# S5 parameter arithmetic (exponentials, angle reduction, powers, unit rotations) issued on GpSimd in place of VectorE

## The chip, the cores and the metric

The kernel runs on one core of a Trainium2 chip. A core has a matrix engine (TensorE; PE in the profile, its weight loads PEld), and three engines for elementwise work: VectorE (DVE), ScalarE (ACT) and GpSimd (POOL); SyncE (SP) issues the DMAs used here. Each engine runs its own instructions strictly in order and waits on semaphores where it needs another engine's result. The metric is the device time of one launch in microseconds (us), lower is better.

## The reference

The program is a trunk of two residual layers over 1024 tokens of width 1024. Layer 0 projects the RMS-normalised input once and runs two branches on it: sliding-window attention with RMS-normalised queries and keys, and an S5 state-space layer. Layer 1 is a sparse attention with a top-k indexer. The change touches only the parameters of S5, which are 32 groups x 64 states:

```
dt = exp(log_dt)[:, None]
mag = exp(a_re * dt)
ang = a_im * dt
ab_re = mag * cos(ang);  ab_im = mag * sin(ang)
den = a_re * a_re + a_im * a_im
f_re = ((ab_re - 1) * a_re + ab_im * a_im) / den
f_im = (ab_im * a_re - (ab_re - 1) * a_im) / den
bb_re = f_re * b_re - f_im * b_im;  bb_im = f_re * b_im + f_im * b_re
x = associative_scan(a complex recurrence with ab over the tokens, driven by bb u)
y = Re(c x) + d_skip * u
```

## The kernel before, in words

All S5 parameters lie as 128 partitions x 16 columns (two states to a partition group), so each elementwise step on them is one instruction on a 128x16 tile. `exp_of` is an exponential written out as elementwise steps: clamp, split off the power of two with a magic constant, range reduction, a polynomial, a rebuilt exponent; 14 instructions on VectorE. It is called twice, for `dt` and, after `tt = a_re*dt`, for `mag`. `ang` is reduced to `r` in [-pi, pi] (`k`, then three fused steps, then a clamp); ScalarE takes sin of `r` and of pi/2-|r|. From `mag`, cos and sin come `P5`, `pw` (the recurrence's factor and its squares) and `ue`, seven unit rotations, each the `square` of the one before, brought back to length one by `unit`. `T16` is built from `ue[0..3]`, `Bb` from `P5`, and both start the S5 quarters (`Q`, `Tb`, `W`, `M`, `X`), the first of which the matrix engine needs at L649.

Around it runs the start of layer 0. Eight pieces of x (1024 tokens x 128) come in by DMA. For each, ScalarE makes `hT_hi` (L335), VectorE the remainder `hT_lo` (L336), and PE multiplies both with the first weights (L356 to L358). The squares (ScalarE, L340) are summed into `acc` (L342), on GpSimd for the first two pieces and on VectorE for the other five. Then one chain leads to the RMS factor of every token:

- PE sums `acc` over partitions (L207), VectorE adds eps (L208), GpSimd raises to -1/2 (L209, `rr`);
- VectorE spreads `rr` on a diagonal (L364, `sq`), PE broadcasts it (L367), ScalarE copies it (L368, `rb`).

PE next projects keys and values, 8 row blocks (L216 to L218, `mm` tiles in three PSUM buffers). Each block's two key heads are normalised by `norm_heads`: squares on ScalarE (L388), then on GpSimd eps (L199), power (L200), factor `rr` (L392); ScalarE scales (L394), which frees the `mm` buffer, and GpSimd applies the gain (L396). Then comes the second chunk of S5's input projection, `u_chunk(1)` (L230 to L232). Weights are split in a high part (ScalarE, L153) and a low part (`wlo`, L154, on VectorE or on GpSimd).

The order of each engine's instructions is fixed when the program is built: a scheduler simulates the program as written, with the `high_priority` blocks first, and writes one list for each engine. The lists decide the rest: an instruction that waits holds all behind it on its engine.

Of the kernel before, what the change touches and what calls it, by code (L numbers as in the profile page):

```python
# [8 lines left out]
F32 = mybir.dt.float32  # L9
# [5 lines left out]
OP = mybir.AluOpType  # L15
# [44 lines left out]
def bc(ap, shape):  # L60
    return ap.to_broadcast(shape)
# [7 lines left out]
def tile_hybrid_swa_s5_dsa(  # L69
# [5 lines left out]
    V, S, G, T = nc.vector, nc.scalar, nc.gpsimd, nc.tensor  # L75
# [159 lines left out]

    MAGIC = 12582912.0

    def exp_of(sp, o, xin, n):

        a, kf, pl = (sp.tile([128, n], F32, name=f"ex{i}", bufs=2) for i in range(3))  # L240
        ki = sp.tile([128, n], I32, name="exi", bufs=2)
        V.tensor_scalar(a, xin, 88.0, -87.0, op0=OP.min, op1=OP.max)
        V.tensor_scalar(kf, a, 1.0 / math.log(2.0), MAGIC, op0=OP.mult, op1=OP.add)
        V.tensor_scalar(kf, kf, MAGIC, None, op0=OP.subtract)
        V.scalar_tensor_tensor(a, kf, -0.693359375, a, op0=OP.mult, op1=OP.add)
        V.scalar_tensor_tensor(a, kf, 0.693359375 - math.log(2.0), a, op0=OP.mult, op1=OP.add)
        V.tensor_scalar(pl, a, 1.0 / 5040.0, None, op0=OP.mult)
        for d_ in (720.0, 120.0, 24.0, 6.0, 2.0, 1.0):
            V.scalar_tensor_tensor(pl, pl, 1.0 / d_, a, op0=OP.add, op1=OP.mult)
        V.tensor_scalar(ki, kf, 127.0, 8388608.0, op0=OP.add, op1=OP.mult)  # L250
        V.scalar_tensor_tensor(o, pl, 1.0, ki.bitcast(F32), op0=OP.add, op1=OP.mult)


    g1r_d = dr.tile([8, FZ], F32, name="g1r_d")
# [41 lines left out]
    sp = es_sp.enter_context(tc.tile_pool(name="s5p", bufs=1, side="right", reuse_waits="tile"))  # L296

    def q16(name):
        return sp.tile([128, 16], F32, name=name)
# [3 lines left out]
    ldt = q16("ldt")  # L303
    with tc.tile_pool(name="x0", bufs=1, reuse_waits="tile") as xp:
# [26 lines left out]
        for k in range(8):  # L331
            xt = xts[k]
            for c in range(0, L, 512 if k == 0 else L):
# [3 lines left out]
                                       op0=OP.mult, op1=OP.subtract)  # L337
# [14 lines left out]
            for half in range(2):  # L352
                for f in range(2):
                    o, hs = ups[2 * f + half], slice(half * 512, half * 512 + 512)
                    a, b = w[0][:, k, f * 128:(f + 1) * 128], w[1][:, k, f * 128:(f + 1) * 128]
# [77 lines left out]
    pw = s5.tile([128, 3, 2, 16], F32, name="pw")  # L433
# [4 lines left out]
    with es_sp:  # L438
        Bre, Bim = Bt[:, 0], Bt[:, 1]
        are, aim = aa[:, 0], aa[:, 1]  # L440
        dt = q16("dt")
        exp_of(sp, dt, ldt, 16)
        tt, ang, k, r = q16("tt"), q16("ang"), q16("k"), q16("r")
        mag, cs, sn, fre, fim = (P5[:, i, :] for i in range(5))
        V.tensor_mul(tt, are, dt)
        exp_of(sp, mag, tt, 16)
        V.tensor_mul(ang, aim, dt)
        V.tensor_scalar(k, ang, 1.0 / (2 * math.pi), MAGIC, op0=OP.mult, op1=OP.add)
        V.tensor_scalar(k, k, MAGIC, None, op0=OP.subtract)
        c1 = 6.28125  # L450
        c2 = 0.0019350051879882812
        c3 = 2 * math.pi - c1 - c2
        V.scalar_tensor_tensor(r, k, -c1, ang, op0=OP.mult, op1=OP.add)
        V.scalar_tensor_tensor(r, k, -c2, r, op0=OP.mult, op1=OP.add)
        V.scalar_tensor_tensor(r, k, -c3, r, op0=OP.mult, op1=OP.add)
        V.tensor_scalar(r, r, 3.1415925, -3.1415925, op0=OP.min, op1=OP.max)
        S.activation(sn, r, AF.Sin)
        V.scalar_tensor_tensor(tt, r, -1.0, r, op0=OP.mult, op1=OP.max)
        V.tensor_scalar(tt, tt, -1.0, math.pi / 2, op0=OP.mult, op1=OP.add)
        S.activation(cs, tt, AF.Sin)  # L460
        den, nre, nim = q16("den"), q16("nre"), q16("nim")
        V.tensor_mul(den, are, are)
        V.tensor_mul(tt, aim, aim)
        V.tensor_add(den, den, tt)
        V.reciprocal(den, den)
        V.tensor_mul(nre, mag, cs)
        V.tensor_scalar(nre, nre, -1.0, None, op0=OP.add)
        V.tensor_mul(nim, mag, sn)
        V.tensor_mul(fre, nre, are)
        V.tensor_mul(tt, nim, aim)  # L470
        V.tensor_add(fre, fre, tt)
        V.tensor_mul(fre, fre, den)
        V.tensor_mul(fim, nim, are)
        V.tensor_mul(tt, nre, aim)
        V.tensor_sub(fim, fim, tt)
        V.tensor_mul(fim, fim, den)
        G.memset(CB, 0.0)
        dma(CT, sc_in)
        V.tensor_scalar(CT[:, 1], CT[:, 1], -1.0, None, op0=OP.mult)


        dma(dsk[96:128], bass.AP(tensor=sd_in.tensor, offset=sd_in.offset, ap=[[0, 32], [1, 512]]))
        dv = dsk[96:128].rearrange("h (q i g) -> h q i g", q=4, g=8)
        GE.tensor_mul(dv, dv,
                      bc(ident[96:128, None, 112:128, None], [32, 4, 16, 8]))

        tm = [sp.tile([128, 256], F32, name=f"tm{i}") for i in range(4)]

        def small(i):
            return tm[i][:, :16]  # L490

        mg, c_, s_ = P5[:, 0], P5[:, 1], P5[:, 2]
        V.tensor_mul(pw[:, 0, 0], mg, c_)
        V.tensor_mul(pw[:, 0, 1], mg, s_)

        def square(dst, src):
            V.tensor_mul(small(0), src[:, 0], src[:, 0])
            V.tensor_mul(small(1), src[:, 1], src[:, 1])
            V.tensor_sub(dst[:, 0], small(0), small(1))
            V.scalar_tensor_tensor(dst[:, 1], src[:, 0], 2.0, src[:, 1], op0=OP.mult, op1=OP.mult)  # L500

        square(pw[:, 1], pw[:, 0])
        square(pw[:, 2], pw[:, 1])
        square(ue[:, 0], P5[:, 1:3])
        square(ue[:, 1], ue[:, 0])
        square(ue[:, 0], ue[:, 1])

        def unit(e):

            V.tensor_mul(small(0), e[:, 0], e[:, 0])  # L510
            V.tensor_mul(small(1), e[:, 1], e[:, 1])
            V.tensor_add(small(0), small(0), small(1))
            V.tensor_scalar(small(0), small(0), -0.5, 1.5, op0=OP.mult, op1=OP.add)
            V.tensor_mul(e, e, bc(small(0)[:, None, :], [128, 2, 16]))

        unit(ue[:, 0])
        for i in range(1, 7):
            square(ue[:, i], ue[:, i - 1])
            unit(ue[:, i])
        V.memset(T16[:, 0, :, 0:1], 1.0)  # L520
        V.memset(T16[:, 1, :, 0:1], 0.0)
        for lv in range(4):
            n = 1 << lv
            er, ei = (bc(ue[:, lv, i, :, None], [128, 16, n]) for i in range(2))
            ts = [t[:, :16 * n].rearrange("p (j n) -> p j n", n=n) for t in tm]
            V.tensor_mul(ts[0], T16[:, 0, :, 0:n], er)
            V.tensor_mul(ts[1], T16[:, 1, :, 0:n], ei)
            V.tensor_mul(ts[2], T16[:, 1, :, 0:n], er)
            V.tensor_mul(ts[3], T16[:, 0, :, 0:n], ei)
            V.tensor_sub(T16[:, 0, :, n:2 * n], ts[0], ts[1])  # L530
            V.tensor_add(T16[:, 1, :, n:2 * n], ts[2], ts[3])
        V.tensor_mul(R8, mg, mg)
        V.tensor_mul(R8, R8, R8)
        V.tensor_mul(R8, R8, R8)
        fr, fi = (bc(P5[:, i, :, None], [128, 16, 16]) for i in (3, 4))
        tmv = [t.rearrange("p (j h) -> p j h", h=16) for t in tm]
        V.tensor_mul(tmv[0], Bre, fr)
        V.tensor_mul(tmv[1], Bim, fi)
        V.tensor_sub(Bb[:, 0], tmv[0], tmv[1])
        V.tensor_mul(tmv[2], Bim, fr)  # L540
        V.tensor_mul(tmv[3], Bre, fi)
        V.tensor_add(Bb[:, 1], tmv[2], tmv[3])
# [264 lines left out]
    for u in range(16 + SWA_AHEAD):  # L807
        if u < 16:
            b, kv = divmod(u, 2)
# [5 lines left out]
        if u >= SWA_AHEAD:  # L815
            b, kv = divmod(u - SWA_AHEAD, 2)
# [39 lines left out]
    for i in range(2):  # L856
        whi, wlo = wstream.get()
        wstream.after = ()
        for half in range(2):
            t0 = half * 512  # L860
            ca = cat[half]
            for n2 in range(2):
                n = 2 * i + n2
                pp = []
                for part in (1, 0):
                    ps = ps_mm.tile([128, 512], F32, name="mm")
                    for k in range(4):
                        a = whi[:, 2 * k + part, n2 * 128:(n2 + 1) * 128]
# [6 lines left out]
                sg = st3.tile([128, 512], F32, name="sg", bufs=4)  # L875
# [18 lines left out]
    for half in range(2):  # L894
# [20 lines left out]
        r = xp1.tile([128, 4], F32, name="r1")  # L915
# [16 lines left out]
    for k in range(0, 8, 3):  # L932
        n = min(3, 8 - k)
# [699 lines left out]
```

## Time and profile before

| what | value |
|---|---|
| median of 3 runs | 1088.2 us (1085.74 to 1091.84) |
| profiled execution | 1088.23 us; its span 1086.5 us, 1.7 us around it |
| busy PE / DVE / ACT / POOL | 1020.1 / 792.8 / 597.2 / 445.9 us |
| TensorE clock granted, mean | 0.976 |

Busy time is the sum over an engine's instructions; the span is from the first to the last instruction of the core. Times in rows count from the start of the span.

### The profile page before, as it was taken

The page shows a single profiled execution, that of the slowest core. Times are in us where ns is not written, and L with a number is a line of the kernel's source. Part 1 is how long each engine was busy: PE and PEld are TensorE (multiplying, and loading weights), DVE is VectorE, ACT ScalarE, POOL GpSimd, SP SyncE. Part 2 cuts the span into 40 slices and gives each one's busy share as a digit, 9 for nine tenths or more (in the row PEclk, how much of TensorE's full clock was granted, in tenths as well). Part 3 has the DMA queues.
Part 4 walks back from the last instruction along what each step waited for, and adds up shares of the span by engine and source line. Part 5 has one row for each costly group of instructions (what it writes and reads, how often), then busy time and mean ns, then how long its engine had stood idle before and what let it go on. Part 6 is the DMA issues. An engine that isn't in the chain of part 4 may idle for free.

```text
span 1086.5 us, 19104 instructions
## 1 busy us (share of the span) xinstructions
PE 1020.1 (94%) x6536; PEld 895.5 (82%) x6536; DVE 792.8 (73%) x1758; ACT 597.2 (55%) x1589; POOL 445.9 (41%) x650
## 2 busy tenths in 40 slices
PE   6898899999999899999799989999997879999998
PEld 4697889999777488878589989999886768988898
DVE  7899798636778554386668578988896988777742
ACT  6453455225546332254455889789935866665520
POOL 2167795232212022144140578767413455445000
PEclk9899899999999999999999999999998999999999
DMA  7283454474323416542012122112336785655323
GB/s 262 78 266 97 128 152 112 148 233 146 116 89 126 136 58 198 199 148 95 1 40 69 64 80 84 40 64 87 105 104 210 224 252 168 194 182 170 106 94 120
DMA packets 109074, 142.52 MB, mean 131 GB/s; under 512 B 9609, under 2 KB 84233, under 8 KB 104113
## 3 DMA queue, kind: packets, MB, share of 16 engines
q1 hardware_dynamic: 108976, 141.31, 41.2%
q8 instruction: 51, 0.84, 0.3%
q14 instruction: 47, 0.38, 0.1%
HBM read 104.41 MB, written 38.31 MB: 131 GB/s over the span
## 4 chain that ended last, share of the span: by engine, by line
PE 68%; DVE 18%; ACT 4%; DMA 4%; issue 3%; POOL 3%; SPq 1%; DVEq 0%; ACTq 0%; POOLq 0%
PE mm L230 8%; PE mm L231 8%; PE mm L232 8%; PE mm L216 4%; PE mm L217 4%; PE mm L218 4%; PE mm L1505 2%; PE mm L1506 2%; PE mm L1504 2%; PE tr L1373 2%; PE psx L799 2%; DVE xh L925 1%; PE pq L1347 1%; DVE tmp L690 1%; PE mm L1388 1%
## 5 line engine op out<-in xcount | busy, mean ns | idle before, releaser
L154 POOL TENSOR_TENSOR wlo<-wraw,whi 128x512 fp32r<-128x512 f32 (+1 forms) x42 | 90.3, 2176 | 104.3 <-ACT whi L153 98.5
L153 ACT CAST whi<-wraw 128x512 fp32r<-128x512 f32 (+2 forms) x120 | 83.7, 755 | 71.8 <-PE mm L231 27.6
L1346 POOL TENSOR_TENSOR bt<-bt,mk 128x384 f32<-128x384 f32 (+3 forms) x80 | 85.0, 1077 | 81.6 <-DMA bt<-g_d 54.6
L216 PE MATMUL mm<-whi,h1T_hi 128*128 128x256 f32 x384 | 110.3, 289 | 0.0
L218 PE MATMUL mm<-whi,h1T_lo 128*128 128x256 f32 x384 | 109.7, 287 | 0.0
L217 PE MATMUL mm<-wlo,h1T_hi 128*128 128x256 f32 x384 | 109.6, 286 | 0.0
L1207 DVE TENSOR_SCALAR_CACHE_REDUCE vjunk<-sc,vt 128x512 bf16<-128x512 uint16 (+5 forms) x90 | 91.1, 1012 | 3.0
L231 PE MATMUL mm<-hT_lo,whi 128*128 128x256 f32 (+1 forms) x288 | 86.3, 300 | 0.0
L232 PE MATMUL mm<-hT_hi,wlo 128*128 128x256 f32 (+1 forms) x288 | 86.3, 300 | 0.0
L230 PE MATMUL mm<-hT_hi,whi 128*128 128x256 f32 (+1 forms) x288 | 85.9, 298 | 0.0
L1241 ACT ACTIVATE sjunk<-sc,st 128x384 bf16<-128x384 uint16 (+5 forms) x90 | 77.3, 859 | 6.4 <-POOL st L1245 4.1
L154 DVE TENSOR_TENSOR wlo<-wraw,whi 128x512 fp32r<-128x512 f32 (+1 forms) x78 | 58.7, 787 | 23.4 <-ACT whi L153 19.1
L1504 PE MATMUL mm<-aT_hi,whi 128*128 128x256 f32 x256 | 73.4, 287 | 1.2 <-ACT aT_hi L1478 1.2
L216 PEld LDWEIGHTS mm<-whi,h1T_hi 128*128 128x128 f32 x384 | 73.1, 191 | 0.6
L1505 PE MATMUL mm<-aT_lo,whi 128*128 128x256 f32 x256 | 72.6, 283 | 0.9 <-DVE aT_lo L1479 0.9
L217 PEld LDWEIGHTS mm<-wlo,h1T_hi 128*128 128x128 f32 x384 | 73.1, 190 | 0.3
L218 PEld LDWEIGHTS mm<-whi,h1T_lo 128*128 128x128 f32 x384 | 72.9, 190 | 0.3
L1506 PE MATMUL mm<-aT_hi,wlo 128*128 128x256 f32 x256 | 72.4, 283 | 0.0
L394 ACT ACTIVATE st<-mm,nr 128x64 f32<-128x64 f32 (+1 forms) x160 | 45.5, 357 | 40.8 <-POOL nr L392 36.7
L1357 ACT ACTIVATE s<-s,mn 128x128 f32<-128x128 f32 (+7 forms) x64 | 49.5, 774 | 29.0 <-DVE mn L1351 29.0
L1064 DVE SCALAR_TENSOR_TENSOR sc<-relu,wi,sc 128x384 f32<-128x384 f32 (+3 forms) x70 | 49.5, 708 | 20.5 <-ACT relu L1059 16.6
L1376 ACT CAST pT_hi<-tr 128x512 fp32r<-128x512 f32 x72 | 41.3, 578 | 37.4 <-PE tr L1373 33.4
(383 smaller groups left out, 3493.4 us busy)
## 6 DMA issues: line engine op xcount, KB each, us to landing
wraw<-in_w_dram SPq DMA_DIRECT2D x20, 1024.0 KB, 5.1
wraw<-in_wo_dram SPq DMA_DIRECT2D x16, 1024.0 KB, 5.1
bt<-g_d SPq DMA_DIRECT2D x24, 256.0 KB, 3.8
g_d<-g1r_d SPq DMA_DIRECT2D x8, 576.0 KB, 10.8
bt<-g_d SPq DMA_DIRECT2D x24, 192.0 KB, 3.5
qT_d<-gst SPq DMA_DIRECT2D x32, 128.0 KB, 2.3
qT<-qT_d SPq DMA_DIRECT2D x32, 128.0 KB, 3.4
xh<-in_xT_dram SPq DMA_DIRECT2D x16, 256.0 KB, 3.2
```

The source lines that it names most:

```text
L154: eng.tensor_sub(lo[p_], raw[p_], rd(hi[p_]))
L216: T.matmul(ps, a, hi[:, k, c0:c1], start=(k == 0), stop=False)
L217: T.matmul(ps, a, lo[:, k, c0:c1], start=False, stop=False)
L218: T.matmul(ps, b, hi[:, k, c0:c1], start=False, stop=(k == 7))
L230: T.matmul(o, a, hT[0][:, k, ts], start=(k == 0), stop=False)
L231: T.matmul(o, a, hT[1][:, k, ts], start=False, stop=False)
L232: T.matmul(o, b, hT[0][:, k, ts], start=False, stop=(k == 7))
L1207: V.tensor_scalar(junk[:, :128 * (b + 1)], data(b), self.thr(j), None, op0=OP.is_ge, op1=OP.add, accum_out=self.cnt[:, it, j:j + 1])
L1346: G.tensor_add(bt, bt, mk[b][:, ks])
L1504: T.matmul(ps, a, aT[0][:, k, toks], start=(k == 0), stop=False)
L1505: T.matmul(ps, a, aT[1][:, k, toks], start=False, stop=False)
L1506: T.matmul(ps, b, aT[0][:, k, toks], start=False, stop=(k == 7))
```

## The change

`exp_of` gets the engine and a fused-step function as arguments, and both calls now run on GpSimd. A fused step (scalar_tensor_tensor), one instruction on VectorE, becomes two on GpSimd, which pass through one shared tile `stt_t`. So one exponential has 23 instructions in place of 14, and a `square` 5 in place of 4. Products with `dt`, the reduction of `ang`, the clamp, pi/2-|r|, `pw`, all `square` and all `unit` go to GpSimd too. |r|, `den`, `nre`, `nim`, `fre`, `fim`, `R8`, `T16` and `Bb` stay on VectorE.

```
-        exp_of(sp, dt, ldt, 16)
+        stt_t = q16("stt_t")
+
+        def g_stt(o, a, c, b, op0, op1):
+            G.tensor_scalar(stt_t, a, c, None, op0=op0)
+            G.tensor_tensor(o, stt_t, b, op=op1)
+
+        exp_of(G, g_stt, sp, dt, ldt, 16)
...
-        V.tensor_mul(tt, are, dt)
-        exp_of(sp, mag, tt, 16)
-        V.tensor_mul(ang, aim, dt)
+        G.tensor_mul(tt, are, dt)
+        exp_of(G, g_stt, sp, mag, tt, 16)
+        G.tensor_mul(ang, aim, dt)
...
-        V.scalar_tensor_tensor(r, k, -c1, ang, op0=OP.mult, op1=OP.add)
...
+        g_stt(r, k, -c1, ang, op0=OP.mult, op1=OP.add)
...
-        V.tensor_mul(pw[:, 0, 0], mg, c_)
-        V.tensor_mul(pw[:, 0, 1], mg, s_)
+        sg_ = [q16(f"sg{i}") for i in range(2)]
+        G.tensor_mul(pw[:, 0, 0], mg, c_)
+        G.tensor_mul(pw[:, 0, 1], mg, s_)
...
         def square(dst, src):
-            V.tensor_mul(small(0), src[:, 0], src[:, 0])
-            V.tensor_mul(small(1), src[:, 1], src[:, 1])
-            V.tensor_sub(dst[:, 0], small(0), small(1))
-            V.scalar_tensor_tensor(dst[:, 1], src[:, 0], 2.0, src[:, 1], op0=OP.mult, op1=OP.mult)
+            G.tensor_mul(sg_[0], src[:, 0], src[:, 0])
+            G.tensor_mul(sg_[1], src[:, 1], src[:, 1])
+            G.tensor_sub(dst[:, 0], sg_[0], sg_[1])
+            g_stt(dst[:, 1], src[:, 0], 2.0, src[:, 1], op0=OP.mult, op1=OP.mult)
...
         def unit(e):
...
-            V.tensor_mul(e, e, bc(small(0)[:, None, :], [128, 2, 16]))
+            G.tensor_mul(sg_[0], e[:, 0], e[:, 0])
+            G.tensor_mul(sg_[1], e[:, 1], e[:, 1])
+            G.tensor_add(sg_[0], sg_[0], sg_[1])
+            G.tensor_scalar(sg_[0], sg_[0], -0.5, 1.5, op0=OP.mult, op1=OP.add)
+            G.tensor_mul(e, e, bc(sg_[0][:, None, :], [128, 2, 16]))
```

The lists differ in the first eighth of the program only. GpSimd's list from the sums of squares to the first key norms, before:

```order
L342 TENSOR_TENSOR acc<-acc,sq 128x1024 x2
L209 TENSOR_TENSOR rr<-rr,neghalf 128x8
L199 TENSOR_SCALAR nr<-nms 128x2
L200 TENSOR_TENSOR nr<-nr,neghalf 128x2
L199 TENSOR_SCALAR nr<-nms 128x2
L392 TENSOR_TENSOR nr<-nr,rr 128x2
```

After the change the same list goes on, behind the second sum, with 72 steps of S5's parameters (both exponentials, `ang`, `r`, `pw`, the first `square` of `ue`); L445 and L446 are the two halves of a fused step. Its end, and what follows:

```order
L445 TENSOR_SCALAR stt_t<-P_386 128x16
L504 TENSOR_TENSOR ue<-sg_498,sg_499 128x16
L446 TENSOR_TENSOR ue<-stt_t,P_386 128x16
L209 TENSOR_TENSOR rr<-rr,neghalf 128x8
L502 TENSOR_TENSOR sg_498<-ue 128x16
L503 TENSOR_TENSOR sg_499<-ue 128x16
...
L518 TENSOR_SCALAR sg_498<-sg_498 128x16
L199 TENSOR_SCALAR nr<-nms 128x2
L519 TENSOR_TENSOR ue<-ue,sg_498 128x32
L200 TENSOR_TENSOR nr<-nr,neghalf 128x2
L199 TENSOR_SCALAR nr<-nms 128x2
```

So L209 now stands behind 72 more instructions, whose work was on VectorE; the first seven key norms are interleaved with the remaining 75 steps of `ue`, and the eighth stands behind them and behind GpSimd's next weight split (L154).

VectorE's list from its last sum of squares to the diagonal L364, after the change (`P_386` is P5):

```order
L342 TENSOR_TENSOR acc<-acc,sq 128x1024
L537 TENSOR_TENSOR R_393<-P_386 128x16
L538 TENSOR_TENSOR R_393<-R_393 128x16
L539 TENSOR_TENSOR R_393<-R_393 128x16
L464 SCALAR_TENSOR_TENSOR tt<-r 128x16
...
L208 TENSOR_SCALAR rr<-tr 128x8
L154 TENSOR_TENSOR wlo<-wraw,whi 128x512 x3
L364 TENSOR_TENSOR sq<-ident,rr 128x1024
```

Before, the sum was followed by the second exponential and the reduction of `ang` on the same engine; now L537 (which reads `mag`) and L464 (which reads `r`) wait there for GpSimd, and L208 stands behind them.

## Rows read from the trace of the kernel before

**Rows 1.** The page's busy time of each engine, share of the span, instructions.

```profile
PE 1020.1 (94%) x6536; PEld 895.5 (82%) x6536; DVE 792.8 (73%) x1758; ACT 597.2 (55%) x1589; POOL 445.9 (41%) x650
```

**Rows 2.** Waits of PE, 10 to 130 us: line, releaser, total, times, longest.

```profile
PE ps L649 <- DVE Q L612: 3.9, 1, 3.9
PE tr L367 <- DVE sq L364: 3.6, 1, 3.6
PE ps L357 <- DVE hT_lo L336: 3.1, 1, 3.1
PE ps L708 <- DMA M<-km: 2.5, 1, 2.5
```

**Rows 3.** Timeline of PE and ACT: start, duration, instruction, idle before and releaser.

```profile
38.05 0.22 ACT L457 ACTIVATE P<-r 128x16 f32<-128x16 f32 x1 [5.86 <-DVE r L456]
38.47 0.22 ACT L460 ACTIVATE P<-tt 128x16 f32<-128x16 f32 x1 [0.20 <-DVE tt L459]
48.15 3.78 PE L367 MATMUL tr<-sq,ones 128*128 128x512 f32 x4 [3.65 <-DVE sq L364]
70.43 0.48 PE L230 MATMUL mm<-hT_hi,whi 128*128 128x512 f32 x1
```

**Rows 4.** Timeline of POOL, 12 to 56 us.

```profile
12.90 4.99 POOL L342 TENSOR_TENSOR acc<-acc,sq 128x1024 f32<-128x1024 f32 x2 [9.06 <-ACT sq L340]
43.98 1.71 POOL L209 TENSOR_TENSOR rr<-rr,neghalf 128x8 f32<-128x8 f32 x1 [26.09 <-DVE pw L499]
49.00 0.26 POOL L199 TENSOR_SCALAR nr<-nms 128x2 f32<-128x2 f32 x1 [3.31 <-ACT st L388]
49.34 0.73 POOL L200 TENSOR_TENSOR nr<-nr,neghalf 128x2 f32<-128x2 f32 x1
```

**Rows 5.** Timeline of DVE, 10 to 48 us.

```profile
13.10 2.38 DVE L462 TENSOR_TENSOR den<-aa 128x16 f32<-128x16 f32 x1
15.60 2.32 DVE L243 TENSOR_SCALAR ex<-ex 128x16 f32<-128x16 f32 x1
18.04 1.28 DVE L336 SCALAR_TENSOR_TENSOR hT_lo<-xt,gain,hT_hi 128x1024 fp32r<-128x1024 f32 x1
...
36.65 0.17 DVE L242 TENSOR_SCALAR ex<-tt 128x16 f32<-128x16 f32 x1
...
46.88 1.22 DVE L364 TENSOR_TENSOR sq<-ident,rr 128x1024 f32<-128x1024 f32 x1
```

**Rows 6.** Groups of POOL by line, 48.5 to 72.3 us: busy, mean ns, idle before.

```profile
L200 POOL TENSOR_TENSOR nr<-nr,neghalf 128x2 f32<-128x2 f32 x7 | 5.1, 729 | 0.4
L396 POOL TENSOR_TENSOR st<-st,kg 128x128 f32<-128x128 f32 x7 | 4.6, 663 | 2.1 <-ACT st L394 1.4 <-DMA g_d<-g1r_d 0.6
L199 POOL TENSOR_SCALAR nr<-nms 128x2 f32<-128x2 f32 x7 | 1.7, 250 | 11.0 <-ACT st L388 10.7
L392 POOL TENSOR_TENSOR nr<-nr,rr 128x2 f32<-128x2 f32 x7 | 1.5, 217 | 0.4
```

**Rows 7.** Window 18 to 36.7 us: its length, then busy PE, PEld, DVE, ACT, POOL.

```profile
18.00:36.70 18.70, 17.32 (x86) 14.79 (x87) 18.52 (x37) 10.22 (x12) 0.00 (x0) 0.91 0.40 139
```

**Rows 8.** Timelines of POOL and DVE at 542 us, and L1243's durations (min/median/max).

```profile
542.11 0.74 POOL L1243 TENSOR_SCALAR sy<-ssum 128x1 f32<-128x1 f32 x1 [3.58 <-ACT sjunk L1241]
541.13 5.03 DVE L1064 SCALAR_TENSOR_TENSOR sc<-relu,wi,sc 128x512 f32<-128x512 f32 x6
L1243 POOL TENSOR_SCALAR sy<-ssum x96: 213/235/740, 542.1 to 793.0; 128x1 f32<-128x1 f32 x96
```

**Rows 9.** Timelines of POOL and DVE, 67 to 72 us.

```profile
67.91 1.81 POOL L396 TENSOR_TENSOR st<-st,kg 128x128 f32<-128x128 f32 x1 [0.63 <-ACT st L394]
67.97 0.41 DVE L537 TENSOR_TENSOR tm<-Bt,P 128x256 f32<-128x256 f32 x1
68.98 0.41 DVE L541 TENSOR_TENSOR tm<-Bt,P 128x256 f32<-128x256 f32 x1
```

**Rows 10.** Waits of PE's weight loads, 52 to 72 us.

```profile
PEld mm L216 <- ACT st L394: 1.4, 1, 1.4
```

More of the change, by code (lines that the diff above doesn't have):

```diff
@@ L236, in tile_hybrid_swa_s5_dsa, with exp_of @@
     MAGIC = 12582912.0
-    def exp_of(sp, o, xin, n):
+    def exp_of(E, stt, sp, o, xin, n):
         a, kf, pl = (sp.tile([128, n], F32, name=f"ex{i}", bufs=2) for i in range(3))
         ki = sp.tile([128, n], I32, name="exi", bufs=2)
[L242 to L247, printed above, removed]
+        E.tensor_scalar(a, xin, 88.0, -87.0, op0=OP.min, op1=OP.max)
+        E.tensor_scalar(kf, a, 1.0 / math.log(2.0), MAGIC, op0=OP.mult, op1=OP.add)
+        E.tensor_scalar(kf, kf, MAGIC, None, op0=OP.subtract)
+        stt(a, kf, -0.693359375, a, op0=OP.mult, op1=OP.add)
+        stt(a, kf, 0.693359375 - math.log(2.0), a, op0=OP.mult, op1=OP.add)
+        E.tensor_scalar(pl, a, 1.0 / 5040.0, None, op0=OP.mult)
         for d_ in (720.0, 120.0, 24.0, 6.0, 2.0, 1.0):
-            V.scalar_tensor_tensor(pl, pl, 1.0 / d_, a, op0=OP.add, op1=OP.mult)
-        V.tensor_scalar(ki, kf, 127.0, 8388608.0, op0=OP.add, op1=OP.mult)
-        V.scalar_tensor_tensor(o, pl, 1.0, ki.bitcast(F32), op0=OP.add, op1=OP.mult)
+            stt(pl, pl, 1.0 / d_, a, op0=OP.add, op1=OP.mult)
+        E.tensor_scalar(ki, kf, 127.0, 8388608.0, op0=OP.add, op1=OP.mult)
+        stt(o, pl, 1.0, ki.bitcast(F32), op0=OP.add, op1=OP.mult)
     g1r_d = dr.tile([8, FZ], F32, name="g1r_d")
@@ L441, in tile_hybrid_swa_s5_dsa @@
         dt = q16("dt")
-        exp_of(sp, dt, ldt, 16)
+        stt_t = q16("stt_t")
[3 more added lines that the diff above has]
+        exp_of(G, g_stt, sp, dt, ldt, 16)
         tt, ang, k, r = q16("tt"), q16("ang"), q16("k"), q16("r")
         mag, cs, sn, fre, fim = (P5[:, i, :] for i in range(5))
-        V.tensor_mul(tt, are, dt)
-        exp_of(sp, mag, tt, 16)
-        V.tensor_mul(ang, aim, dt)
-        V.tensor_scalar(k, ang, 1.0 / (2 * math.pi), MAGIC, op0=OP.mult, op1=OP.add)
-        V.tensor_scalar(k, k, MAGIC, None, op0=OP.subtract)
+        G.tensor_mul(tt, are, dt)
+        exp_of(G, g_stt, sp, mag, tt, 16)
+        G.tensor_mul(ang, aim, dt)
+        G.tensor_scalar(k, ang, 1.0 / (2 * math.pi), MAGIC, op0=OP.mult, op1=OP.add)
+        G.tensor_scalar(k, k, MAGIC, None, op0=OP.subtract)
         c1 = 6.28125
@@ L452, in tile_hybrid_swa_s5_dsa @@
         c3 = 2 * math.pi - c1 - c2
-        V.scalar_tensor_tensor(r, k, -c1, ang, op0=OP.mult, op1=OP.add)
-        V.scalar_tensor_tensor(r, k, -c2, r, op0=OP.mult, op1=OP.add)
-        V.scalar_tensor_tensor(r, k, -c3, r, op0=OP.mult, op1=OP.add)
-        V.tensor_scalar(r, r, 3.1415925, -3.1415925, op0=OP.min, op1=OP.max)
+        g_stt(r, k, -c1, ang, op0=OP.mult, op1=OP.add)
+        g_stt(r, k, -c2, r, op0=OP.mult, op1=OP.add)
+        g_stt(r, k, -c3, r, op0=OP.mult, op1=OP.add)
+        G.tensor_scalar(r, r, 3.1415925, -3.1415925, op0=OP.min, op1=OP.max)
         S.activation(sn, r, AF.Sin)
         V.scalar_tensor_tensor(tt, r, -1.0, r, op0=OP.mult, op1=OP.max)
-        V.tensor_scalar(tt, tt, -1.0, math.pi / 2, op0=OP.mult, op1=OP.add)
+        G.tensor_scalar(tt, tt, -1.0, math.pi / 2, op0=OP.mult, op1=OP.add)
         S.activation(cs, tt, AF.Sin)
+        tt = q16("t2")
         den, nre, nim = q16("den"), q16("nre"), q16("nim")
@@ L487, in tile_hybrid_swa_s5_dsa @@
         tm = [sp.tile([128, 256], F32, name=f"tm{i}") for i in range(4)]
-        def small(i):
-            return tm[i][:, :16]
         mg, c_, s_ = P5[:, 0], P5[:, 1], P5[:, 2]
-        V.tensor_mul(pw[:, 0, 0], mg, c_)
-        V.tensor_mul(pw[:, 0, 1], mg, s_)
+        sg_ = [q16(f"sg{i}") for i in range(2)]
+        G.tensor_mul(pw[:, 0, 0], mg, c_)
+        G.tensor_mul(pw[:, 0, 1], mg, s_)
         def square(dst, src):
-            V.tensor_mul(small(0), src[:, 0], src[:, 0])
-            V.tensor_mul(small(1), src[:, 1], src[:, 1])
-            V.tensor_sub(dst[:, 0], small(0), small(1))
-            V.scalar_tensor_tensor(dst[:, 1], src[:, 0], 2.0, src[:, 1], op0=OP.mult, op1=OP.mult)
+            G.tensor_mul(sg_[0], src[:, 0], src[:, 0])
+            G.tensor_mul(sg_[1], src[:, 1], src[:, 1])
+            G.tensor_sub(dst[:, 0], sg_[0], sg_[1])
+            g_stt(dst[:, 1], src[:, 0], 2.0, src[:, 1], op0=OP.mult, op1=OP.mult)
         square(pw[:, 1], pw[:, 0])
@@ L508, in unit @@
         def unit(e):
[L510 to L513, printed above, removed]
-            V.tensor_mul(e, e, bc(small(0)[:, None, :], [128, 2, 16]))
+            G.tensor_mul(sg_[0], e[:, 0], e[:, 0])
[3 more added lines that the diff above has]
+            G.tensor_mul(e, e, bc(sg_[0][:, None, :], [128, 2, 16]))
         unit(ue[:, 0])
```

## The prediction

> **What bounds the kernel now.** I read the busy times first: PE works for 1020 of 1086.5 us [rows 1]. A change that makes nothing for PE can therefore save only where PE waits, and costs wherever it makes PE wait longer. The lists of the change differ in the first 130 us alone, so the waits of PE there come second [rows 2]: 3.1 us for the second `hT_lo`, 3.6 us for L364 (the RMS factor), 2.5 and 3.9 us in the start of S5. Those are all that could be won, some 13 us, and only the first two, 6.7 us, lie ahead of or in the RMS chain.
>
> Third, the timelines around the RMS chain. GpSimd is idle for 26 us between its sums and L209, while VectorE goes without a gap (18.52 of 18.7 us busy, GpSimd 0.00) [rows 4, 7]. That looks like free room for S5's arithmetic. But L209 is a link of the chain for which PE already waits: L209 from 43.98 to 45.69, L364 at 46.88, L367 on PE at 48.15 [rows 3 to 5]. The room on GpSimd thus has a deadline, 43.98, and the new list puts 72 instructions ahead of it. What those cost decides the case.
>
> **The price of one GpSimd step.** The trace before has no 128x16 step on GpSimd. The nearest rows are the key norms on 128x2: a tensor_scalar 0.25 us, a tensor_tensor 0.217 us [rows 6], and 0.08 us from the end of one to the start of the next that depends on it (49.00 + 0.26 to 49.34) [rows 4]. Almost all the steps depend on the one before, and the two kinds are about equally many: (0.25 + 0.217)/2 + 0.07 = 0.30 us. On VectorE a step took 0.17 and issues overlapped [rows 5]. From below, without the gap, a step is 0.23 us.
>
> That price holds where VectorE leaves GpSimd alone. At 542 us it doesn't: L1243 took 0.74 us, when its usual time is 0.235, beside VectorE's L1064, six instructions in 5.03 us, 0.84 each, with several SBUF inputs [rows 8]. The GpSimd step ended at 542.85, right after the second of them (541.13 + 2 x 0.84 = 542.81): it had waited for the VectorE instruction that ran. A worse row is L396 at 67.91, 1.81 us [rows 9], where the six others of that form took (4.6 - 1.81)/6 = 0.47 [rows 6]; it lasted through L537 to L541 on VectorE, four instructions between 67.97 and 69.39 [rows 9]. The other direction shows too: while GpSimd summed two squares (4.99 us), VectorE's 128x16 steps of 0.17 us took 2.38 and 2.32 us [rows 4, 5].
>
> The Trainium skill says on its page "SBUF — State Buffer", section "Who interferes with whom", that VectorE instructions with two SBUF inputs and GpSimd instructions that read SBUF share one read interface, and that whoever issues first holds it for its whole instruction. The 0.74 us above agrees; the 1.81 us is more than that rule gives. By the rule GpSimd gets one step in after each VectorE instruction, which is the sum below; by the longer hold the sum would be the rival named starvation.
>
> **The sum, step by step.** (1) GpSimd's two sums and first three steps end about 18.1 (before: 12.90 + 4.99 = 17.89 for the sums alone [rows 4]). (2) From there VectorE has its stream of wide instructions, `hT_lo` (1.28 us each), sums, weight splits, all with two SBUF inputs: about 22 instructions in the new list. Before, it ran from 18.04 to 36.65 [rows 5] with a dozen small steps that go, about 1 us; the two stalls of 2.4 and 2.3 us go partly, and a GpSimd step let in between two instructions costs some 0.1 us each. I take its end as 37. One GpSimd step for each: 22 of the 54 that lead to the clamped `r` are done by then. (3) The other 32 at 0.30 us take 9.6 us: `r` at 46.6. (4) The two sines with |r| and pi/2-|r| between took 0.64 us (38.05 to 38.69 [rows 3]); with the handing over to and from GpSimd I take 0.9: 47.5. (5) `pw` and the first `square`, 17 steps: 5.1 us, to 52.6. L208 stands on VectorE behind |r| and eleven small steps, ready by about 49, so it isn't late for this. (6) L209 itself, 1.71 us: 54.3, against 45.69 before. (7) Before, L364 began 1.2 us after L209's end, since weight splits stood ahead of it; now they are done in the wait. L364 at 54.4, against 46.88: **+7.5 us** for PE at L367.
>
> (8) Behind L209 GpSimd has 75 steps of `ue` and seven key norms: 75 x 0.29 + 7 x 1.9 (0.73 + 0.66 + 0.25 + 0.22 [rows 6] and gaps) = 35 us. Before, the norms filled 12.9 of 23.8 us there, and 11.0 more were waits for ScalarE [rows 6]. The norms now come late by growing amounts, up to 7 or 8 us after L209; L394 then frees the `mm` buffers late. PE is already held once by them, 1.4 us [rows 10], so with three buffers the lateness passes to PE: the second projection chunk, at 70.43 before [rows 3], slips by about 5 us more than L209 did. In step with it, `T16` waits on VectorE for `ue[1..3]`, and `W`, `M` and `Q` come 5 to 7 us later, which meets PE's waits at L708 and L649 [rows 2]; these waits shift with their sources and hide little of it. I take **+5 us**.
>
> (9) VectorE loses some 120 small steps, about 10 us of its time; the stretch in which that could help PE is (2), and the gain ends before the wait for L209, so it counts for nothing. Behind 130 us the lists are alike and PE is nearly full, so what is late there stays late. Sum: 7.5 + 5 = 12.5 on the profiled execution's 1088.23, which stands at the median of the three runs (1088.2): **1101 us**.
>
> **Bounds.** L209's end is 45.69 if the 72 steps fit in the room, and 18.1 + at most 19 us of starvation + 72 x 0.30 + 0.9 + 1.7 = 61 if VectorE lets none in. The tail is worth 2 to 8 us.
>
> **Rivals.**
> - *Starvation.* GpSimd gets fewer than one step for each wide VectorE instruction, as L396 did [rows 9]. With none, L209 ends 61, L364 +14, and with the tail +19: 1107. With VectorE's own stream also slowed it could be 1112. Against it: L396's own form is 128x128 and longer.
> - *No contention.* If steps of 128x16 slip between VectorE's wide instructions at 0.30 us, the 72 end at 18.1 + 21.6 + 0.9 = 40.6, ahead of 43.98, and L209 is on time; only the tail is left: +4 to +6, 1093. For it: no row shows a 128x16 GpSimd step beside a 1024-wide VectorE one; against it rows 8.
> - *The other side: same or faster.* The stalls of 2.4 and 2.3 us on VectorE [rows 5] are what makes the second `hT_lo` late and PE wait 3.1 us [rows 2]; they go, and if L209 is in time, PE is 3 us ahead at L367. If the norms also keep up, the kernel ends at 1083 to 1088. It decides at a step's price, waits included, of (43.98 - 18.1 - 0.9)/72 = 0.35 us: below, L209 is on time, above it's late by 72 times the excess. The least price found is 0.23, with rows 8 more than double that while VectorE streams.
>
> **Chances.** The forecast (1095 to 1106 by itself) 0.66; starvation 0.09; no contention with a late tail 0.16; same or faster 0.09. A measurement of this kernel tells about 0.5%, 5.4 us, from no change. Below 1082.8 lies a third of the last case, 0.03; within 1082.8 to 1093.6 the rest of it and half of the third, 0.14; slower 0.83. The range leaves out most of the last case and the end of starvation: 1091 to 1109.
>
> **What would show it.** Steps 2 and 3: GpSimd's 128x16 steps at 0.7 to 1.3 us between 18 and 37, at 0.2 to 0.3 after; the first sine at 46 to 48 instead of 38.05. Step 6: L209 starts at 51 to 54 instead of 43.98. Step 7: PE idles some 11 us ahead of L367 instead of 3.65. Step 8: key norms without idle time for ScalarE on GpSimd, PE waits for L394, the second chunk at 82 to 84 instead of 70.43, L649 about 12 us later than before. I'm wrong if L209 starts before 46 (then 0.30 us held throughout), if PE's waits at L708 and L649 shrink to nothing (then the tail was hidden), or if a list behind 130 us moved.

## The result, and the profile after

The changed kernel takes 1094.5 us (median of 7 runs, 1090.9 to 1099.4) against 1086.7 us for the kernel before beside it: ratio 1.0079, interval 1.0057 to 1.0101, so it is slower by 6 to 11 us (8.6 by the ratio, 7.8 by the medians). The profiled execution took 1094.36 us. In the changed kernel's file lines from about L510 on stand five lower than before: L649 is L654 there, L708 is L713.

GpSimd's timeline around and behind its second sum, and its groups by line between the end of that sum and the end of VectorE's wide stream (21.8 to 36.8 us):

```profile
13.93 0.58 POOL L242 TENSOR_SCALAR ex<-ldt 128x16 f32<-128x16 f32 x1 [10.10 <-DMA ldt<-in_ldt_dram]
18.45 3.36 POOL L342 TENSOR_TENSOR acc<-acc,sq 128x1024 f32<-128x1024 f32 x1
21.89 1.12 POOL L445 TENSOR_SCALAR stt_t<-ex 128x16 f32<-128x16 f32 x1
...
36.81 0.25 POOL L445 TENSOR_SCALAR stt_t<-ex 128x16 f32<-128x16 f32 x1
37.15 0.22 POOL L446 TENSOR_TENSOR ex<-stt_t,ex 128x16 f32<-128x16 f32 x1
...
48.32 0.20 POOL L462 TENSOR_SCALAR r<-r 128x16 f32<-128x16 f32 x1
...
53.73 1.67 POOL L209 TENSOR_TENSOR rr<-rr,neghalf 128x8 f32<-128x8 f32 x1
```

```profile
L445 POOL TENSOR_SCALAR stt_t<-ex 128x16 f32<-128x16 f32 x7 | 6.8, 978 | 0.6
L446 POOL TENSOR_TENSOR ex<-stt_t,ex 128x16 f32<-128x16 f32 x7 | 5.2, 736 | 0.6
```

The same step takes 0.25 or 0.22 us when VectorE is idle and 0.98 or 0.74 on the mean while VectorE streams. Between 21.89 and 36.81 only 16 steps got through; the other 38 up to `r` took 11.7 us, 0.31 each. L209 starts at 53.73, where it started at 43.98 [rows 4].

What stands behind it on VectorE and PE, and all waits of PE between 10 and 130 us:

```profile
46.34 0.17 DVE L537 TENSOR_TENSOR R<-P 128x16 f32<-128x16 f32 x1 [9.69 <-POOL P L446]
55.43 1.23 DVE L364 TENSOR_TENSOR sq<-ident,rr 128x1024 f32<-128x1024 f32 x1 [2.49 <-POOL rr L209]
```

```profile
56.72 3.53 PE L367 MATMUL tr<-sq,ones 128*128 128x512 f32 x4 [13.70 <-DVE sq L364]
82.42 0.47 PE L230 MATMUL mm<-hT_hi,whi 128*128 128x512 f32 x1
```

```profile
PE tr L367 <- DVE sq L364: 13.7, 1, 13.7
PE ps L713 <- DMA M<-km: 3.1, 1, 3.1
PE ps L356 <- ACT hT_hi L335: 3.0, 1, 3.0
PE mm L216 <- ACT st L394: 2.6, 1, 2.6
PE ps L654 <- DVE Q L617: 2.2, 1, 2.2
```

Set against [rows 2, 3], L367 is 8.6 us late (56.72 against 48.15) and the second projection chunk 12.0 (82.42 against 70.43): a wait for a key norm (L394, 2.6 us) came on top, and 0.9 us that PE lost around that wait, when its granted clock was at 0.50, the lower of its two levels (1.2 of 2.4 GHz), a second time (63.3 to 66.7 us). Then some comes back: the wait at L654 is 2.2 us where it was 3.9, and PE keeps its full granted clock behind it (1.00), where before, behind waits of 2.5 and 3.9 us, it ran at a granted 0.63 (window 119 to 127.5 us; 0.50 up to 123.5). The wait gives back 1.7 us and the clock about 2.6: at 134 us PE is 7.6 late. At 150 us a query norm holds it (L407 for L394, 2.9 us, and a granted clock of 0.50 to 155 us), so it is 12.2 late; the kernel before has two waits of its own at 144 and 154 us (1.0 and 0.9) that are missing here, and at 239 us PE is 10.3 late. The rest of this one pair of executions takes it to 6.1; the medians differ by 7.8.

VectorE's lines behind the shorter wait, first in the changed kernel, then (L542, L581, L612) before:

```profile
74.47 0.41 DVE L547 TENSOR_TENSOR Bb<-tm,tm 128x256 f32<-128x256 f32 x1
79.79 0.68 DVE L586 TENSOR_TENSOR kT<-tr,kT 64x512 fp32r<-64x512 f32 x1 [4.91 <-ACT kT L585]
129.18 0.41 DVE L617 TENSOR_TENSOR Q<-tmp 128x256 f32<-128x256 f32 x1
```

```profile
67.17 0.68 DVE L581 TENSOR_TENSOR kT<-tr,kT 64x512 fp32r<-64x512 f32 x1
70.75 0.42 DVE L542 TENSOR_TENSOR Bb<-tm,tm 128x256 f32<-128x256 f32 x1
118.66 0.42 DVE L612 TENSOR_TENSOR Q<-tmp 128x256 f32<-128x256 f32 x1
```

Here `Bb` is done before VectorE gets the keys (kT) from ScalarE, and VectorE even waits for them; before, `Bb` stood behind them. From kT to Q it takes 49.4 us, where it took 51.5.

### The profile page after: what moved, and what is told of

It is laid out like the page before. It is cut to its first block, busy times and chain, and to the rows that moved or that the text cites. A ratio compares the mean times of both kernels' runs of the same rounds, so it can differ in the third digit from the quotient of the medians.

```text
span 1092.6 us, 19143 instructions
## 1 busy us (share of the span) xinstructions
PE 1016.7 (93%) x6536; PEld 893.1 (82%) x6536; DVE 779.6 (71%) x1640; ACT 597.6 (55%) x1589; POOL 487.7 (45%) x800
## 4 chain that ended last, share of the span: by engine, by line
PE 63%; DVE 13%; POOL 11%; ACT 4%; issue 4%; DMA 3%; SPq 1%; DVEq 0%; ACTq 0%; POOLq 0%
PE mm L231 8%; PE mm L232 8%; PE mm L230 7%; PE mm L216 4%; PE mm L217 4%; PE mm L218 4%; PE mm L1510 2%; PE mm L1511 2%; PE mm L1509 2%; POOL wlo L154 2%; PE tr L1378 2%; PE psx L804 2%; DVE xh L930 1%; DMA bt<-g_d 1%; POOL stt_t L445 1%
## 5 line engine op out<-in xcount | busy, mean ns | idle before, releaser
L154 POOL TENSOR_TENSOR wlo<-wraw,whi 128x512 fp32r<-128x512 f32 (+1 forms) x42 | 90.3, 2175 | 102.7 <-ACT whi L153 91.4
L232 PE MATMUL mm<-hT_hi,wlo 128*128 128x256 f32 (+1 forms) x288 | 86.4, 300 | 0.0
L154 DVE TENSOR_TENSOR wlo<-wraw,whi 128x512 fp32r<-128x512 f32 (+1 forms) x78 | 60.0, 807 | 23.0 <-ACT whi L153 18.9
L216 PEld LDWEIGHTS mm<-whi,h1T_hi 128*128 128x128 f32 x384 | 72.3, 189 | 0.6
L394 ACT ACTIVATE st<-mm,nr 128x64 f32<-128x64 f32 (+1 forms) x160 | 45.3, 354 | 43.6 <-POOL nr L392 38.8
L1381 ACT CAST pT_hi<-tr 128x512 fp32r<-128x512 f32 x72 | 41.4, 578 | 34.4 <-PE tr L1378 30.2
```

What stands on the lines that cost most here:

```text
L154: eng.tensor_sub(lo[p_], raw[p_], rd(hi[p_]))
L216: T.matmul(ps, a, hi[:, k, c0:c1], start=(k == 0), stop=False)
L232: T.matmul(o, b, hT[0][:, k, ts], start=False, stop=(k == 7))
```

## The experiments

Two theories of the loss stand against each other. Theory A: L209 stands on GpSimd behind S5's steps and comes late. Theory B: the steps behind L209 share GpSimd with the key norms and make these late (the tail). The cuts of code below are shortened.

For each run the table gives the start of L209, the start of L367 on PE, how late PE starts the same matmul at 239 us (the L232 that starts at 239.17 before; all PE lists have it in the same place), and the ratio to the kernel before.

| run | L209 at | L367 at | late at 239 | ratio, interval |
|---|---|---|---|---|
| before | 43.98 | 48.15 | 0 | 1 |
| the change | 53.73 | 56.72 | 10.3 | 1.0079 (1.0057 to 1.0101) |
| e1_exp_only | 51.57 | 55.01 | 12.6 | 1.0086 (1.0069 to 1.0102) |
| e2_ue_only | 43.93 | 47.80 | 11.4 | 1.0120 (1.0091 to 1.0150) |
| e3_rr_first | 39.44 | 42.91 | 10.3 | 1.0081 (1.0059 to 1.0103) |
| e4_ldt_early | 48.56 | 51.55 | 10.9 | 1.0162 (1.0144 to 1.0181) |
| p_e1 | 52.52 | 56.65 | 8.3 | 1.0073 (1.0052 to 1.0094) |
| p_e2 | 44.52 | 48.39 | 5.7 | 1.0074 (1.0053 to 1.0094) |
| p_w1 | 53.15 | 56.31 | 7.4 | 1.0075 (1.0055 to 1.0095) |
| c_e2 | 44.89 | 49.06 | 4.8 | 1.0059 (1.0034 to 1.0084) |
| f_l1 | 43.94 | 47.77 | -4.3 | 0.9996 (0.9968 to 1.0023) |
| f_q3 | 42.10 | 46.22 | -3.8 | 0.9969 (0.9945 to 0.9993) |
| f_q1 | 42.52 | 46.47 | -4.5 | 0.9986 (0.9960 to 1.0013) |
| f_q34 | 40.91 | 45.03 | 0.9 | 1.0009 (0.9986 to 1.0033) |

**First set: halves of the change, the order on GpSimd, an earlier start.**

e1_exp_only keeps `exp_of(G, ...)` and gives `pw`, `square` and `unit` back to `V`; e2_ue_only does the opposite.

> Both exponentials, the angle and its reduction stay on GpSimd; the powers, square and unit are back on VectorE. Theory A (the time is lost because L209 stands on GpSimd behind S5's steps): r is ready as late as with the whole change, about 48 us, L208 and L209 follow at about 51 instead of 53.7, so PE's L367 comes about 5 us late, and VectorE has its ue steps again, so nothing is given back later: ratio to the kernel before 1.004 to 1.007. Theory B (the time is lost in the tail, because ue and the key norms share GpSimd behind L209): nothing of the tail is left, 1.000 to 1.002.

> Only the powers, square and unit are on GpSimd; the exponentials and the angle are back on VectorE. Theory A: r at about 38 us as before, few steps ahead of L209, which starts by 46; PE's L367 is less than 2 us late, and VectorE's relief from ue shortens PE's waits at the start of S5 by 2 to 4 us: ratio 0.996 to 1.001. Theory B: the tail on GpSimd is whole, so most of the loss stays: 1.005 to 1.008.

In e3_rr_first the change gets two lines (`behind` only sets the order of issue on that engine):

```
+            rr_ins = mean_square(acc, 8, rr[:, 0])   # returns L209's instruction
+        with behind([rr_ins]):                       # from tt and the second exponential to the last unit
             G.tensor_mul(tt, are, dt)
```

> The whole change, but on GpSimd all from the second exponential on is issued behind L209. Theory A: L209 starts at 44 to 46, PE's L367 is less than 2 us late; the angle, powers and ue come some 8 us later than in the change, which PE pays in part at L654: ratio 1.000 to 1.005, faster than the change. Theory B: the work on GpSimd behind L209 grows from 35 to 50 us, so the loss is as large as with the change or larger: 1.008 or more.

e4_ldt_early moves the three loads of `ldt` and `aa` ahead of x and the weights, and puts `behind([last sum])` around VectorE's steps from |r| to R8.

> The whole change, but log_dt and a are loaded ahead of x and the weights, so that GpSimd starts its steps at about 5 us instead of 13.9, before VectorE's wide stream; VectorE's steps that wait for GpSimd (|r|, R8 and what follows) are issued behind its last sum of squares. Theory A with contention: some 30 steps run at 0.3 us ahead of the stream, L209 starts at 44 to 47, and the loss is gone or turned to a small gain: ratio 0.997 to 1.002. If the price of a step is not the contention with VectorE but high throughout, L209 starts at 50 or later: 1.004 or more. Theory B: 1.006 to 1.008, since the tail is untouched.

L209 and L367 came within 2 us of where theory A put them in e1 and e2, and earlier still in e3. The times did not follow: with L367 on time (e2) or 5 us early (e3) the kernels are as slow as the change, or slower, and PE is 10 to 11 us late at 239 us. Neither A nor B gave all of that. A missed e2 and e3. B was met in e3 (1.0081), but had 1.008 at most for e2 and 1.002 at most for e1, which had no tail. e4 met no expectation (1.0162, L209 at 48.56). A further cause shows in the lists: in the changed kernel those of ScalarE and SP are those of before but for some 40 instructions, while in e1 to e4 the scheduler, which had other ready times to work with, re-sorted all five lists over most of layer 0's first half. So a third theory, D: part of these times is the new lists, not the work moved. e4's time can't be read for contention for that reason, and its x arrives later too (PE's first matmul at 7.95 us, 6.03 before). Its trace can: GpSimd's 128x16 steps took 0.20 to 0.27 us from 3.9 to 7.0 us, ahead of VectorE's stream, and mostly 0.5 to 1.3 us from 20 to 37 us, beside it.

**Second set: the lists held.** These kernels chain the instructions of every engine, S5's parameter steps aside, in the order in which they stand in the program before (for the first 260 us; in the third set to the end):

```
+    for a_, b_ in zip(row_, row_[1:]):          # row_: one engine's instructions in the order of before
+        tc.add_manual_dep(b_, a_.name, NoSync)  # order of issue only, no wait
```

p_e1 and p_e2 are e1 and e2 so held. c_e2 is the reverse: the kernel before, all on VectorE, held in the lists of e2.

> The work of e1_exp_only (exponentials and angle on GpSimd, the rest on VectorE), but every other instruction of the first 260 us is held in the order in which it stands in the kernel before; only S5's own parameter steps find their places anew. In e1_exp_only the scheduler had re-sorted all lists. Theory A (L209's lateness): L209 at about 51.5 us, PE's L367 some 6 us late, ratio 1.004 to 1.006. Theory D (the re-sorted lists cost, not the work moved): the ratio falls well below the 1.0086 of e1_exp_only, to 1.003 or less. If neither: 1.0086 again.

> The work of e2_ue_only (powers, square, unit on GpSimd), all other instructions held in the order of the kernel before. Theory A: L209 is on time, VectorE is relieved of ue: 0.997 to 1.002. Theory B (the tail, ue and key norms sharing GpSimd): 1.005 to 1.012, as in e2_ue_only. Theory D: well below the 1.012 of e2_ue_only, 1.003 or less, by A or not.

> The work of the kernel before, nothing moved to GpSimd, but all instructions outside S5's parameters held in the order that the scheduler had chosen for e2_ue_only. Theory D: a good part of e2_ue_only's 1.012 is there, 1.005 or more. If the lists are innocent: 0.998 to 1.002.

p_w1 leaves S5 on VectorE and makes only L209 late:

```
+        dm = xp.tile([128, 8], F32, name="dm")
+        last = G.tensor_tensor(dm, acc[:, :8], neghalf[:, :8], op=OP.pow)   # waits for the last sum
+        for _ in range(8):
+            last = G.tensor_tensor(dm, dm, neghalf[:, :8], op=OP.pow)
-        with tc.high_priority():
+        with tc.high_priority(), behind([last.ins]):
             mean_square(acc, 8, rr[:, 0])
```

> The kernel before, its lists held, S5's arithmetic on VectorE as before; nine powers of 128x8 that nobody reads are put on GpSimd between the end of the sum of squares and L209, so that L209 starts at about 53 instead of 44 and nothing else is changed. Theory A: PE is 8 to 9 us late at L367 and stays so: 1.006 to 1.010; as VectorE has no relief here, not less than the whole change (1.0079). If L209's lateness is made good later (S5's start waits less): 1.000 to 1.004. Theory B: 1.000 to 1.003.

p_w1's GpSimd, and its waits of PE from 10 to 130 us (L450 is L367 there, L736 L649, L436 L357, L795 L708):

```profile
37.09 1.70 POOL L439 TENSOR_TENSOR dm<-acc,neghalf 128x8 f32<-128x8 f32 x1 [18.91 <-DVE ex L321]
38.87 14.32 POOL L441 TENSOR_TENSOR dm<-dm,neghalf 128x8 f32<-128x8 f32 x8
53.15 1.63 POOL L288 TENSOR_TENSOR rr<-rr,neghalf 128x8 f32<-128x8 f32 x1
```

```profile
PE tr L450 <- DVE sq L447: 11.6, 1, 11.6
PE ps L736 <- DVE Q L699: 3.9, 1, 3.9
PE ps L436 <- DVE hT_lo L415: 3.1, 1, 3.1
PE ps L795 <- DMA M<-km: 2.2, 1, 2.2
```

Each of these waits but the one for L364 is within 0.3 us of [rows 2], and PE's lateness is 8.2 us at L367 and between 7.3 and 8.1 at every place up to 240 us. A late L209 by itself is worth the whole result: 1.0075. That is A, shown with nothing else moved. p_e1 behaves like it (8.0 us flat). D, which had 1.003 or less for it, missed: 1.0073 against 1.0086 of e1, a difference that the intervals don't show.

p_e2 has L209 on time and is as slow, 1.0074, which neither A (1.002 at most) nor D (1.003) allowed. Its waits of PE, 45 to 200 us (L485 is L407, L472 and L474 are L394 and L396, L661 the transpose of the keys, L735 L649):

```profile
PE tr L485 <- ACT st L472: 6.3, 4, 2.4
PE tr L445 <- DVE sq L442: 3.4, 1, 3.4
PE tr L661 <- POOL st L474: 3.0, 2, 2.4
PE mm L294 <- ACT st L472: 2.5, 1, 2.5
PE ps L735 <- DVE Q L698: 2.2, 1, 2.2
PE ps L794 <- DMA M<-km: 1.7, 1, 1.7
```

The waits for key and query norms (L472, L474) make 11.8 us; before, the query norms cost PE 1.5 us up to 200 us, and the key norms held its weight loads for 1.4 [rows 10]. Two waits at the start of S5 are shorter, by 1.7 and 0.8 us [rows 2]. So B holds too: some 80 steps on GpSimd among the norms cost more than the relief of VectorE gives. And c_e2 shows D at work in e2: with no work moved, e2's lists cost 1.0059. In its trace PE waits 10.7 us for query norms from 45 to 200 us, and not at all for Q:

```profile
PE tr L485 <- ACT st L472: 10.7, 4, 3.6
```

e2's 1.0120 is about p_e2's work and c_e2's lists together (1.0074 x 1.0059 = 1.0133).

**Third set: what there was to win, and a better version.** All lists held to the end.

> What there was to win: the kernel before with its lists held, in which the arithmetic that the change moves is left out (each exponential is one instruction that writes 0.5, each square a copy, unit nothing), so neither VectorE nor GpSimd does it, and the output is not the reference's. If VectorE's small steps bound the start of S5, as the change supposes: 0.990 to 0.995. If PE's waits there have other causes: 0.996 to 1.000; then a move to another engine, which can't be better than leaving out, had at most 4 us to win.

f_q3 changes one order on VectorE (`lo_ins` holds the instructions of L336):

```
+        with behind([lo_ins[3]]):               # the hT_lo of k = 2
             exp_of(sp, dt, ldt, 16)             # ... to V.reciprocal(den, den)
```

> The kernel before, lists held, nothing on GpSimd; VectorE's first seven parameter steps, which stall behind GpSimd's two sums (2.4 and 2.3 us) with the second hT_lo behind them, are issued behind the hT_lo of k = 2. If that stall is what PE's wait of 3.1 us at 19.4 us is made of, PE is 1.5 to 3 us early from there on and stays so, as p_w1's lateness stayed: 0.997 to 0.9985. If GpSimd's sums hold hT_lo itself back as long, or L364 waits for weight splits anyway: 0.999 to 1.001.

f_q1 takes the change's first exponential alone (`exp_of(G, g_stt, sp, dt, ldt, 16)`), with VectorE's steps from `tt` on `behind` its last sum; f_q34 is f_q3 with `square` and `unit` of ue[4..6] on GpSimd.

> The kernel before, lists held, with the first exponential alone on GpSimd (23 steps between its sums and 38 us) and VectorE's other parameter steps behind its last sum of squares; L209 stands behind 23 steps that end before it can start. Theory A: nothing is late at L209, and VectorE has no stall ahead of hT_lo: 0.997 to 0.9995. If GpSimd's steps beside VectorE's wide stream cost VectorE as much as they save: 1.000 to 1.003.

> f_q3, and in addition ue[4..6] (the last three squares and units, 30 steps, first read at about 80 us) on GpSimd among the key norms. If VectorE's relief of some 4 us ahead of Q shortens PE's waits at L708 and L649 (2.5 and 3.9 us) and 30 steps fit in GpSimd's waits for ScalarE (11 us there): 0.994 to 0.998, better than f_q3. Theory B (what shares GpSimd with the key norms makes them late): worse than f_q3 by 0.002 or more.

Leaving the moved arithmetic out gains nothing that the runs can tell: 0.9996, and by its interval at most 0.3%. It left the waits of PE as they were (L591 is L357 there, L880 L649), and VectorE idle ahead of the keys (L812 is L581):

```profile
PE ps L591 <- DVE hT_lo L570: 3.2, 1, 3.2
PE ps L880 <- DVE Q L843: 3.8, 1, 3.8
66.49 0.68 DVE L812 TENSOR_TENSOR kT<-tr,kT 64x512 fp32r<-64x512 f32 x1 [8.00 <-ACT kT L811]
```

The stall ahead of `hT_lo` stays, since the next steps on VectorE take the place of those left out. The time won behind it goes into a wait of 8.0 us for ScalarE's keys: L812 starts 0.7 us earlier than before. In the held list the end of `T16` and `Bb` stands behind that wait, so f_l1 tells what the relief brings in this order, not in every one. f_q3 gets past it, VectorE's timeline (L582 is L336, L487 is L242):

```profile
15.01 2.62 DVE L582 SCALAR_TENSOR_TENSOR hT_lo<-xt,gain,hT_hi 128x1024 fp32r<-128x1024 f32 x1 [0.70 <-ACT hT_hi L581]
17.55 2.38 DVE L487 TENSOR_SCALAR ex<-ldt 128x16 f32<-128x16 f32 x1
```

Now `hT_lo` itself stands beside a sum on GpSimd and takes 2.62 us, not 1.28 [rows 5], but ends at 17.6, not 19.3, and the 2.4 us stall lies behind it. PE has no wait there, starts L367 1.9 us earlier and keeps that to 100 us. 0.9969 (0.9945 to 0.9993): f_q3 beats both kernels, the one before by little more than the noise, with nothing of S5 on GpSimd. It is not shown to beat f_l1: the medians of both are the same (1083.5 and 1083.3 us, before 1086.7), and f_l1's profiled execution is as early at 239 us. f_q1 is within noise of before; its 23 steps on GpSimd end at 37.0 us, ahead of L209. f_q34 is 3.1 us early at L367 and has lost that by 90 us (PE waits 1.6 and 0.7 us for key norms and 1.2 for Q); then it waits 2.4 us for a query norm at 141 us, and ends 0.4% behind f_q3 (medians 1088.0 and 1083.5 us of 12 runs each; the intervals against before overlap by 0.0007). That is what B expected, with only 30 steps.

## Why the prediction was right, and where it was off

The time, 1094.5 us, lies within the stated 1091 to 1109, but just below the 1095 to 1106 that the forecast gave itself, and nearer to the rival *no contention* (1093) than to 1101. So the time alone would not tell which of the two held; the trace does.

- **Steps 2 and 3, contention.** One GpSimd step for each wide VectorE instruction, then 0.30 us each. Measured: 16 of the 22 that I had, the sums ending at 21.8 instead of 18.1 (the load of `ldt` came at 13.9, and VectorE's stream took its share of the second sum, 3.36 us against 2.5), and 0.31 us afterwards. VectorE's stream ended at 36.65, forecast 37. `r` at 48.5, forecast 46.6. The rivals *no contention* (0.30 throughout) and *starvation* (none let in) are both out. The Trainium skill says on its page "SBUF — State Buffer", section "Who interferes with whom", that a VectorE instruction with two SBUF inputs contends with a GpSimd instruction that reads SBUF; the trace agrees (0.98 and 0.74 us against 0.25 and 0.22); a hold as long as the 1.81 us of [rows 9] did not come back.
- **Steps 4 to 7, L209.** Sines and 17 steps took 5.2 us from 48.5 (forecast 6.0); L209 at 53.73 (52.6), L364 8.6 us late (7.5), PE's wait 13.7 us (11). p_w1 shows that this lateness alone gives the result.
- **Step 8, the tail.** This is the term that was mis-sized: +5 us forecast; 3.4 measured at the second projection chunk (12.0 less the 8.6 of L367), 1.7 at 239 us (10.3 less 8.6), and nothing in the times, where the ratio gives 8.6 us in all (6 to 11 by its interval) and L364's lateness is 8.6. That 12.0 us came so near to the forecast 12.5 is luck in part: L364 was 1.1 us later than forecast and the tail shorter (30.2 us and not 35 passed on GpSimd from L209 to the last of the seven norms). And I let it stand to the end. PE got back 4.4 us at L654 and behind it (12.0 to 7.6). Of this 1.7 us is the shorter wait for Q: there VectorE's relief counts, which step 9 took for nothing because it looked at (2) alone. About 2.6 us is the granted clock, which stayed at 1.00 where it had been 0.63. Then the query norms took most of it again. Hence 1101 forecast, 1094.5 measured. That what is late at 130 us stays late (step 9) held only roughly: in this pair 10.3 us at 239 us became 6.1 at the end, in p_w1 7.4 became 8.1.
- **The relief of VectorE**, the reason one would make this change, gave at most 0.3% where the order was held (f_l1); what PE waited for at 19.4 us was an order, not the amount of work (f_q3).

That A and B do not add up in the whole change (1.0075, 1.0074, together 1.0079) is seen but only argued: in the change the norms' lateness meets PE when it is late already, and VectorE has all the relief. No run had both lists held and L209 on time with the whole of the work on GpSimd. Why c_e2's lists make the query norms late was not taken apart.

## What to carry to other kernels

Idle time of an engine is room only up to the next link of the critical chain that this engine holds: look for the deadline in its list, price the moved steps with the neighbour's contention, and ask what is queued behind them. Before moving work to relieve an engine, leave the work out once, with the lists held: if the time hardly falls, the amount of that engine's work is not what the kernel waits for in this order. It is no strict bound, since a move changes the order too, and an order alone can gain (f_q3). And where a scheduler orders the program, hold the lists when parts of a change are compared; otherwise the new order is measured with the work.

## What the runs showed of the hardware that was not expected

GpSimd's short steps cost VectorE's wide stream almost nothing: from its first sum of squares to the end of its last it took 13.8 us (22.82 to 36.65), before 14.2 (22.52 to 36.73) with six steps of 0.17 us more in it. They themselves were stretched three- to fourfold (0.98 and 0.74 us against 0.25 and 0.22). The loss lay on the side of the short instructions. With GpSimd's long sums it was the other way round: VectorE's 0.17 us steps took 2.38 us before, and in the change an `hT_lo` of 1.28 us took 3.43 beside the second sum.
